# Branch a's gates started one to two heads earlier, norm factors on GpSimd and weights read in blocks, in a hybrid attention and mixture-of-experts block

## Chip, cores and metric

The kernel runs on one core of one Trainium2 chip. The metric is the device time of one execution in microseconds (us). Engines are named as in the profile: PE is TensorE, DVE is VectorE, ACT is ScalarE, POOL is GpSimd, SP is SyncE, which here only issues DMAs.

## What is computed

One layer of an encoder over L = 528 tokens (512 and 16 meta tokens) of width 1024. A normalised input `u` goes through one wide projection, its columns feed two attention branches and two gates, the gated branches are added, and a mixture of 16 experts follows.

```python
u = rms_norm(h, g_mix)
z = einsum('bld,df->blf', u, w_in)                     # 1024 x 6656
qa, ka, va, qb, kb, vb, ga, gb = split(z)
oa = diff_attention(qa, ka, va, ...)                   # 8 heads, two softmax maps each
oa = rms_norm(oa, g_subln) * (1 - lam_init)
qh = axial_rope(rms_norm(qb, g_qnorm), ...)            # 8 heads
kh = axial_rope(rms_norm(kb, g_knorm), ...)            # 2 key heads
ob = gqa_attention(qh, kh, vb)
ya, yb = oa @ w_branch_a, ob @ w_branch_b
merged = sigmoid(ga) * ya + sigmoid(gb) * yb
h = h + merged @ w_out
h = h + expert_choice_ffn(rms_norm(h, g_ffn), ...)
```

## The kernel before

**Data.** Activations lie transposed: 128 features on the partitions, 528 tokens along the free axis. Products keep float32 accuracy by splitting each factor into a high and a low part, so a projection of 128 columns is 2 halves of tokens (256 and 272) by 8 chunks by 3 products: 48 matmuls (`project`). Its weight, 128 columns of a matrix, is loaded by SP into `wraw` (`load_weights`), split by ACT into `wh` and by POOL, sometimes DVE, into `wl` (`split_weights`), one projection ahead.

**Stages.** First the input rows are normalised and transposed. Then come eight differential heads (`head_a`), then eight grouped-query heads (`head_b`), then the gates of branch b that are left, the products with `w_branch_b` and `w_out`, the routing, and the experts. While a head's scores and softmax run, PE is given projections as fill: `mix(main, fill, nfill, steps)` lets the head go on by one step when a share of the fill has been issued. A differential head is filled with the q, k and v of the next; the last one with q, v and k of the first grouped-query head. A grouped-query head h is filled with the q of the next, with the gate of branch a for block h (`gate_a(h)`) and with the product of that block with `w_branch_a` (`branch_a(h)`); the first also with the second k and v. The last one takes `gate_a(7)`, `branch_a(7)`, `gate_b(0)`; `gate_b(1)` follows, and six gates stand in the next stage.

**Order.** A recording layer (`Pace`) keeps a modelled clock for each engine and decides from it in which order instructions are written to the engines' queues. Each engine then runs its queue in order; what is late in fact is waited for, with everything behind it.

**Norm factors.** A head's output (and each q and k of branch b) is divided by a root of a mean square. `norm` sums the squares on PE (`sqh`, `sql` with `sel`), has ACT copy the sums to `rows`, has PE transpose them (`ptr<-ident,rows`), and writes mean square plus epsilon to the first column block of `cols5` (named `cols` in the profile, 128 by 5). `rsqrt` then makes the factor there: a bit trick and three Newton steps, 11 small DVE instructions. With `spread`, PE transposes the factors back across the partitions (`pz<-ident,cols`), and DVE multiplies them in. There are 18 such norms: 8 of differential heads and 2 of keys with `spread`, 8 of queries without.

**Buffers.** The tag `m1` first holds `biases` (two buffers of four rows of 528), the distance penalties of the differential heads, head h in buffer h mod 2; after the last head it is taken over for `m1`, the eight gated blocks of branch a. A gate is written by ACT to a tile of tag `f2`, a tag that the heads use too.

Of the kernel before, what the change touches and what calls it, by code (L numbers as in the profile page):

```python
# [20 lines left out]
P = 128  # L21
# [9 lines left out]
NH = 8  # L31
# [38 lines left out]
def keys(ap):  # L70

    kind = ap.name.split("_")[0]
    step = ap.ap[0][0]
    width = {"kbuf": L, "biases": 4 * L, "h2T": L, "xin": D, "pair": L, "obf": L, "hrow": D, "junk": D, "big": D, "first": D, "raw": D,
             "hid": FF // 2, "hhl": 2 * CAP, "xg": 4 * CAP}.get(kind, step)
# [187 lines left out]
class Engines:  # L263
# [7 lines left out]
    hf=1, kr=1, b0="qvkgy", b1="qgy", bn="qgy", zz="f1", bk=0, sp=0, step=6, fa=38, fa7=40, fb=40, fb2=48,  # L271
# [21 lines left out]
def block_kernel(ctx: ExitStack, tc: tile.TileContext, x, meta_tokens, g_mix, w_in,  # L293
                 lambda_q1, lambda_k1, lambda_q2, lambda_k2, g_subln, g_qnorm, g_knorm,
                 w_branch_a, w_branch_b, w_out, g_ffn, w_router, w_gate, w_up, w_down,
# [4 lines left out]
    w_in = w_in[0]  # L300
    wa, wb, wo = w_branch_a[0], w_branch_b[0], w_out[0]
# [30 lines left out]
    cols5 = [const.tile([P, 4, 5], F32, name=f"cols5{i}") for i in range(3)]  # L332
# [132 lines left out]
    def load_weights(j):  # L465
        if j < len(stream) and j not in loaded:
            w, c0 = stream[j]
# [45 lines left out]

    order = []
    for h in range(NH):
        order += [("qa", w_in, C_QA + h * P), ("ka", w_in, C_KA + h * P), ("va", w_in, C_VA + h * P)]
    cols_of = dict(q=("qb", w_in, C_QB), k=("kb", w_in, C_KB), v=("vb", w_in, C_VB))
    order += [cols_of[c] for c in K["o7"]]
    for h in range(NH):
        cols_of = dict(q=("qb", w_in, C_QB + (h + 1) * P), k=("kb", w_in, C_KB + P), v=("vb", w_in, C_VB + P),  # L520
                       g=("ga", w_in, C_GA + h * P), y=("ya", wa, h * P))
        order += [cols_of[c] for c in (K[("b0", "b1", "bn")[min(h, 2)]] if h + 1 < NH else "gy")]
    for d in range(NC):
        order.append(("gb", w_in, C_GB + d * P))
    for d in range(NC):
        order.append(("yb", wb, d * P))
    for d in range(NC):
        order.append(("wo", wo, d * P))
    stream += [(w, c) for _, w, c in order]
# [10 lines left out]
    sel = pb.tile([P, 2, P], F32R, name="sel")  # L540
    vmeta = [pb.tile([P, P], F32R, name=f"vm{i}") for i in range(2)]
# [87 lines left out]
    biases = keep.tile([P, 2, 4, L], F32, tag="m1", name="biases")  # L629
# [8 lines left out]
    nc.gpsimd.tensor_copy(ones, onef)  # L638
    for q in qmeta:
        nc.gpsimd.memset(q.bitcast(F32), 0.0)  # L640
# [105 lines left out]
    def norm(sh, sl, done, spread, sums):  # L746
# [28 lines left out]
        rsqrt(y, a, t_, c[:, 3, :])  # L775
# [264 lines left out]
    def chain(*gens):  # L1040
        for g in gens:
            yield from g

    for h in range(NH):
# [8 lines left out]
    m1 = keep.tile([P, NC, L], F32, tag="m1", name="m1")  # L1053
# [45 lines left out]
    def gate(j, tag="f2", bufs=1, place=None):  # L1099
        box = {"g": place}  # L1100

        def evac(hf, cs, ps):
            if box["g"] is None:
                box["g"] = ftile(tag, "gate", bufs)
            nc.scalar.activation(box["g"][:, cs], ps, AF.Tanh, scale=0.5)
        yield from project(j, u_h, u_l, evac)
        return box["g"]

    def gate_a(d):
        gates_b["a", d] = yield from gate(jof["ga", d], place=obf[:, NH - 1, :] if d == 0 and K["gp"] else None)  # L1110

    def branch_a(d):
        g = gates_b["a", d]

        def evac(hf, cs, ps):
# [8 lines left out]
    def gate_b(d, place=None):  # L1124
        gates_b[d] = yield from gate(jof["gb", d], *(("f0", 2) if d == 1 else ("f2", 1)), place)

    for h in range(NH):
        if h + 1 < NH:
            todo = dict(q=lambda: proj_q(h + 1), k=lambda: proj_k(1), v=lambda: proj_v(1),
                        g=lambda: gate_a(h), y=lambda: branch_a(h))  # L1130
            fill = chain(*[todo[c]() for c in K[("b0", "b1", "bn")[min(h, 2)]]])
        else:
            fill = chain(gate_a(h), branch_a(h), gate_b(0))
        mix(head_b(h), fill, K['fb2'] if h < 2 else K['fb'], K['stb'])
# [5 lines left out]
    through(gate_b(1))  # L1140
# [95 lines left out]
    places += [ftile("sqh", "gate"), ftile("f1", "gate")]  # L1236
    for d, place in enumerate(places, 2):
        through(gate_b(d, place))
# [491 lines left out]
    for i in range(4):  # L1730
# [7 lines left out]

_INS = ['x', 'meta_tokens', 'g_mix', 'w_in', 'lambda_q1', 'lambda_k1', 'lambda_q2', 'lambda_k2',
        'g_subln', 'g_qnorm', 'g_knorm', 'w_branch_a', 'w_branch_b', 'w_out', 'g_ffn', 'w_router',  # L1740
# [22 lines left out]
```

## Time and profile before

| | |
|---|---|
| median of 3 runs | 1073.41 us (1071.48 to 1073.82) |
| the profiled execution's own time | 1074.43 us |
| its span, first to last instruction | 1072.7 us |
| PE busy | 969.4 us, 90% of the span |
| DVE, ACT, POOL busy | 758.2, 630.8, 338.7 us |
| mean granted TensorE clock | 0.968 of full speed |
| DMA | 186.44 MB, 174 GB/s over the span |

The span is the time between the first and the last instruction of that execution; 1.7 us lie around it. A busy share says nothing of the end by itself: what counts is where PE, which carries most of the chain that ended last, stands idle, for whom it waits there, and at which clock it runs.

### The profile page before, as it was taken

The numbers are of one execution on the slowest core, as the hardware profiler recorded it, in microseconds if no ns is written. First come the engines' busy times: TensorE is split into PE (matmuls) and PEld (weight loads), VectorE is DVE, ScalarE is ACT, GpSimd is POOL, SyncE is SP. The second block draws the span as 40 slices with busy tenths as digits, with TensorE's granted clock in tenths as the row PEclk, the third lists the DMA queues.
The fourth block names the chain that finished last, engine by engine and source line by source line (L and its number), as shares of the span: only waits on it lengthen the run. The fifth ranks groups of instructions, "written<-read, shape, count | busy, mean of one in ns | idle before, by whom it ended". The sixth has DMA issues, their size and how long they took to land.

```text
span 1072.7 us, 18211 instructions
## 1 busy us (share of the span) xinstructions
PE 969.4 (90%) x6835; PEld 836.1 (78%) x6835; DVE 758.2 (71%) x1550; ACT 630.8 (59%) x1297; POOL 338.7 (32%) x306
## 2 busy tenths in 40 slices
PE   4799999999968999999999999985499999999984
PEld 4799998999958989999999999974256666666562
DVE  5367788887785677676656145566389999999885
ACT  5366666665745455555545433334288888888773
POOL 3232322322312322333223234432223333323153
PEclk9899999999989999999999999998699999999997
DMA  8544444443111222222222545915899999999964
GB/s 246 166 126 109 124 122 119 130 126 100 55 51 42 66 62 71 69 56 65 70 60 83 160 157 171 328 73 201 237 301 376 324 381 328 381 342 361 349 182 184
DMA packets 127502, 186.44 MB, mean 174 GB/s; under 512 B 6298, under 2 KB 84263, under 8 KB 127414
## 3 DMA queue, kind: packets, MB, share of 16 engines
q1 hardware_dynamic: 101046, 87.96, 27.5%
q0 software_dynamic: 25760, 95.16, 26.2%
q10 hardware_dynamic: 608, 2.16, 0.7%
q8 instruction: 54, 0.88, 0.3%
q14 instruction: 34, 0.28, 0.1%
HBM read 162.07 MB, written 10.76 MB: 161 GB/s over the span
## 4 chain that ended last, share of the span: by engine, by line
PE 57%; DVE 21%; ACT 9%; DMA 5%; issue 5%; SPq 1%; POOL 1%; POOLq 0%; ACTq 0%; DVEq 0%
PE pz L199 33%; PE psc L199 19%; PE ptr L199 5%; DVE sn L199 4%; DVE cols L199 3%; ACT sn L199 2%; DVE ls L199 2%; DVE pb L199 2%; SPq L199 1%; DVE wtl L199 1%; DMA raw<-in_w_down_dram 1%; DVE hl L199 1%; DVE nmb L199 1%; DVE ql L199 1%; DVE zb L199 1%
## 5 line engine op out<-in xcount | busy, mean ns | idle before, releaser
L199 POOL TENSOR_TENSOR wl<-wraw,wh 128x512 fp32r<-128x512 f32 x139 | 190.6, 1381 | 475.2 <-ACT wh L199 453.1
L199 PE MATMUL pz<-u_h,wh 128*128 128x256 f32 (+1 forms) x832 | 247.2, 297 | 5.4 <-ACT u_h L199 2.3
L199 PE MATMUL pz<-u_h,wl 128*128 128x256 f32 (+1 forms) x832 | 238.6, 287 | 1.1 <-POOL wl L199 1.1
L199 PE MATMUL pz<-u_l,wh 128*128 128x256 f32 (+1 forms) x832 | 238.4, 287 | 0.4 <-DVE u_l L199 0.4
L199 DVE TENSOR_TENSOR el<-raw,eh 128x1024 fp32r<-128x1024 f32 x180 | 214.0, 1229 | 6.0 <-ACT eh L199 4.9
L199 ACT CAST eh<-raw 128x1024 fp32r<-128x1024 f32 x180 | 182.0, 1049 | 23.5 <-PE pz L199 14.9
L199 PEld LDWEIGHTS pz<-u_h,wh 128*128 128x128 f32 x832 | 158.8, 191 | 8.3 <-DVE kbuf L199 2.7
L199 PEld LDWEIGHTS pz<-u_h,wl 128*128 128x128 f32 x832 | 158.5, 190 | 1.3 <-POOL wl L199 1.3
L199 PEld LDWEIGHTS pz<-u_l,wh 128*128 128x128 f32 x832 | 158.8, 191 | 0.6 <-DVE u_l L199 0.6
L199 PE MATMUL psc<-eh,xh 128*66 128x512 f32 (+1 forms) x272 | 105.0, 386 | 2.7 <-ACT hid L199 2.2
L199 ACT CAST wh<-wraw 128x512 fp32r<-128x512 f32 x152 | 91.0, 617 | 24.2 <-PE pz L199 10.9
L199 PE MATMUL psc<-el,xh 128*66 128x512 f32 (+1 forms) x272 | 104.1, 383 | 0.9 <-DVE el L199 0.9
L199 PE MATMUL psc<-eh,xl 128*66 128x512 f32 (+1 forms) x272 | 104.0, 382 | 0.0
L199 DVE TENSOR_TENSOR wtl<-ptr,wth 128x512 fp32r<-128x512 f32 (+1 forms) x72 | 45.9, 637 | 46.7 <-ACT wth L199 46.1
L199 ACT ACTIVATE sn<-sn,nm 128x528 f32<-128x528 f32 x64 | 47.1, 736 | 47.0 <-DVE nm L199 46.4
L199 PE MATMUL pz<-eh,hhl 128*66 128x512 f32 x224 | 70.7, 396 | 0.6 <-DVE hhl L199 0.6
L199 POOL DMA_INDIRECT acc<-ys,idxu x15 | 28.8, 1921 | 119.8 <-ACT ys L199 117.5
L199 ACT CAST wth<-ptr 128x512 fp32r<-128x512 f32 (+1 forms) x72 | 39.0, 542 | 46.0 <-PE ptr L199 45.5
L199 PEld LDWEIGHTS psc<-eh,xh 128*66 128x66 f32 x272 | 37.5, 138 | 25.4 <-ACT hid L199 3.2
L199 PEld LDWEIGHTS psc<-el,xh 128*66 128x66 f32 x272 | 37.3, 137 | 24.4 <-DVE el L199 1.4
L199 PEld LDWEIGHTS psc<-eh,xl 128*66 128x66 f32 x272 | 37.4, 138 | 21.9 <-issue 0.6
L199 DVE CUSTOM_DVE_ANT_0 sn<-psc,biases 128x528 f32<-128x528 f32 x64 | 44.3, 694 | 6.2 <-PE psc L199 6.2
(311 smaller groups left out, 2352.2 us busy)
## 6 DMA issues: line engine op xcount, KB each, us to landing
wraw<-in_w_in_dram SPq DMA_DIRECT2D x52, 512.0 KB
raw<-in_w_gate_dram POOLq DMA_DIRECT2D x13, 2048.0 KB, 18.5
raw<-in_w_down_dram POOLq DMA_DIRECT2D x13, 2048.0 KB, 15.4
raw<-in_w_up_dram POOLq DMA_DIRECT2D x13, 2048.0 KB, 20.4
biases<-in_c_bias_dram SPq DMA_DIRECT2D x8, 1056.0 KB
kbuf<-kbuf SPq DMA_DIRECT2D x32, 132.0 KB
wraw<-in_w_branch_a_dram SPq DMA_DIRECT2D x8, 512.0 KB
wraw<-in_w_branch_b_dram SPq DMA_DIRECT2D x8, 512.0 KB
```

The lines of the kernel that those rows point to most:

```text
L199: op.fn(*op.args, **op.kw)
```

## The change

1. `gate_a(0)` and `gate_a(1)` join the fill of the last differential head, behind q, v and k; its `nfill` goes from 40 to 32. A grouped-query head h then takes `gate_a(h + 1)` from head 1 on, the last takes `branch_a(7)`, `gate_b(0)`, `gate_b(1)`, and `gate_b(2)`, `gate_b(3)` follow. Four gates are left for the next stage. So block d's gate is projected one head sooner, and block 1's two heads sooner.
2. `m1` is there from the start, with `biases` as a view of it; a gate of branch a is written into the row of `m1` that `branch_a` then multiplies in place. Rows 0 and 1 lie where the even heads' penalties lay, which the last head (7) does not use.
3. `norm` calls `root` on POOL, 5 instructions: a power of -1/2 by `halfs`, and one Newton step.
4. `w_in`, `w_branch_a`, `w_branch_b` and `w_out` are put side by side on the host and cut into blocks of 128 columns, so that a partition reads 4 KB in one piece where it read 8 pieces of 512 bytes.

```diff
 K: fa7=40 -> fa7=32
+    def root(y, a, t):
+        nc.gpsimd.tensor_tensor(y, a, halfs[:, :a.shape[1]], op=OP.pow)
+        nc.gpsimd.tensor_mul(t, y, y)
+        nc.gpsimd.tensor_mul(t, t, a)
+        nc.gpsimd.tensor_scalar(t, t, -0.5, 1.5, op0=OP.mult, op1=OP.add)
+        nc.gpsimd.tensor_mul(y, y, t)
...
-            nc.sync.dma_start(raw, w[:, c0:c0 + P].rearrange("(c p) f -> p c f", p=P))
+            nc.sync.dma_start(raw, w_cols[stream[j]])
...
-    biases = keep.tile([P, 2, 4, L], F32, tag="m1", name="biases")
+    m1 = keep.tile([P, NC, L], F32, tag="m1", name="m1")
+    biases = m1.rearrange("p (a i) l -> p a i l", a=2)
...
-        rsqrt(y, a, t_, c[:, 3, :])
+        root(y, a, t_)
...
+    def gate_a(d):
+        yield from gate(jof["ga", d], place=m1[:, d, :])
...
-            fill = chain(*[dict(k=proj_k, q=proj_q, v=proj_v)[c](0) for c in K["o7"]])
+            fill = chain(*[dict(k=proj_k, q=proj_q, v=proj_v)[c](0) for c in K["o7"]], gate_a(0), gate_a(1))
...
-            nc.vector.scalar_tensor_tensor(m1[:, d, cs], g[:, cs], 1.0, ps, op0=OP.add, op1=OP.mult)
+            nc.vector.scalar_tensor_tensor(m1[:, d, cs], m1[:, d, cs], 1.0, ps, op0=OP.add, op1=OP.mult)
...
-        gates_b[d] = yield from gate(jof["gb", d], *(("f0", 2) if d == 1 else ("f2", 1)), place)
+        tags = ("f2", 1), ("f0", 2), ("sqh", 1), ("f1", 1)
+        gates_b[d] = yield from gate(jof["gb", d], *tags[d % 4], place)
...
-    through(gate_b(1))
+    through(gate_b(2))
+    through(gate_b(3))
...
+def column_blocks(*mats):
+    wide = np.concatenate([m.reshape(NC, P, -1) for m in mats], axis=2)
+    return np.ascontiguousarray(wide.reshape(NC, P, -1, P).transpose(2, 1, 0, 3))
```

**PE at the end of the last differential head.** Here `rows` are the sums of squares of the first key (their transposes), `cols` the factors, `psc<-kbh,qh` the first grouped-query scores, and `pz<-u_h,wh` a projection's matmuls. Before:

```order
L199 MATMUL pz<-u_h,wh 128x256
L199 MATMUL pz<-u_l,wh 128x256
L199 MATMUL pz<-u_h,wl 128x256
L199 MATMUL ptr<-ident,rows_93 128x128 x2
L199 MATMUL ptr<-ident,rows_93 16x128
L199 MATMUL pz<-ident,cols_82 128x128 x5
L199 MATMUL psc<-kbh_201,qh 128x264
L199 MATMUL psc<-kbl_202,qh 128x264
L199 MATMUL psc<-kbh_201,ql 128x264
L199 MATMUL psc<-kbh_201,qh 128x264
```

Now, at the key's factors (`cols_82` here):

```order
L199 MATMUL pz<-u_l,wh 128x256
L199 MATMUL pz<-u_h,wl 128x256
L199 MATMUL pz<-ident,cols_82 128x128 x4
L199 MATMUL pz<-u_h,wh 128x256
L199 MATMUL pz<-u_l,wh 128x256
L199 MATMUL pz<-u_h,wl 128x256
L199 MATMUL pz<-u_h,wh 128x256
L199 MATMUL pz<-u_l,wh 128x256
L199 MATMUL pz<-u_h,wl 128x256
L199 MATMUL pz<-u_h,wh 128x272
```

Before, the key's factors (`cols_82`) came straight behind the key's sums and the first scores straight behind the factors, with no projection between. Now 24 matmuls of the gates stand between those sums and the key's factors (the rows show the end of them), and 18 more of a gate, the last head's 26 products with its values and 12 more of a gate stand between the factors and the first scores.

**DVE and POOL in a steady differential head, at the norm of the head before.** DVE before, from the sums (`sums`) to the end of the factor:

```order
L199 TENSOR_TENSOR sums_83<-sums_83 128x5
L199 SCALAR_TENSOR_TENSOR cols_81<-sums_83,ptr 128x4
L199 SCALAR_TENSOR_TENSOR cols_81<-sums_83,ptr 16x1
L199 TENSOR_SCALAR cols_81<-cols_81 128x5 x2
L199 TENSOR_TENSOR cols_81<-cols_81 128x5 x2
L199 SCALAR_TENSOR_TENSOR cols_81<-cols_81 128x5
L199 TENSOR_TENSOR cols_81<-cols_81 128x5 x2
L199 SCALAR_TENSOR_TENSOR cols_81<-cols_81 128x5
L199 TENSOR_TENSOR cols_81<-cols_81 128x5 x2
```

POOL now, in such a head (`wl` is a weight's low part, `qmeta` a copy for the meta queries):

```order
L199 TENSOR_TENSOR wl<-wraw,wh 128x512
L199 TENSOR_TENSOR cols_82<-cols_82,halfs 128x5
L199 TENSOR_TENSOR cols_82<-cols_82 128x5
L199 TENSOR_TENSOR wl<-wraw,wh 128x512
L199 TENSOR_TENSOR cols_82<-cols_82 128x5
L199 TENSOR_SCALAR cols_82<-cols_82 128x5
L199 TENSOR_TENSOR cols_82<-cols_82 128x5
L199 TENSOR_TENSOR wl<-wraw,wh 128x512 x3
```

The 11 instructions of the root left DVE; the 5 that replace them stand on POOL among the weight splits, with one split inside the chain.

## Rows read from the trace of the kernel before

**Rows 1.** The page: its span, and the chain's shares by engine.

```profile
span 1072.7 us, 18211 instructions
...
PE 57%; DVE 21%; ACT 9%; DMA 5%; issue 5%; SPq 1%; POOL 1%; POOLq 0%; ACTq 0%; DVEq 0%
```

**Rows 2.** Busy time by stretch: bounds, length, busy (instructions) of each engine, clock, DMA.

```profile
302.05:359.32 57.27, 45.70 (x329) 42.94 (x329) 38.69 (x114) 28.91 (x74) 14.92 (x11) 0.88 0.18 50
359.32:396.06 36.74, 34.06 (x279) 33.24 (x277) 24.29 (x64) 16.67 (x42) 9.84 (x7) 1.00 0.24 68
455.40:484.54 29.14, 28.55 (x236) 27.78 (x233) 20.37 (x51) 15.98 (x42) 9.65 (x7) 1.00 0.24 65
```

**Rows 3.** PE's waits from 302 to 360 us: total, times, longest.

```profile
PE pz L199 <- DVE cols L199: 5.2, 1, 5.2
PE pz L199 <- ACT zv L199: 2.5, 1, 2.5
```

**Rows 4.** Timeline at the change of stages: start, us, engine, operation, [idle before <-releaser].

```profile
306.38 0.49 PE L199 MATMUL ptr<-ident,rows 128*128 128x128 f32 x3
...
306.78 2.48 POOL L199 TENSOR_TENSOR wl<-wraw,wh 128x512 fp32r<-128x512 f32 x2 [12.35 <-DMA zp<-zb]
...
308.11 2.43 DVE L199 TENSOR_TENSOR cols<-cols 128x5 f32<-128x5 f32 x2
...
312.09 1.09 PE L199 MATMUL pz<-ident,cols 128*128 128x128 f32 x4 [5.22 <-DVE cols L199]
```

**Rows 5.** Groups on DVE, the root's products: xcount, busy us, mean ns.

```profile
L199 DVE TENSOR_TENSOR cols<-cols 128x5 f32<-128x5 f32 x108 | 26.4, 246 | 2.0
...
L199 DVE SCALAR_TENSOR_TENSOR cols<-cols 128x5 f32<-128x5 f32 x54 | 8.8, 164 | 1.4
```

**Rows 6.** Groups on POOL, by shape.

```profile
L199 POOL TENSOR_TENSOR wl<-wraw,wh 128x512 fp32r<-128x512 f32 x139 | 190.6, 1381 | 475.2 <-ACT wh L199 453.1 <-DMA zp<-zb 14.9 <-PE ptr L199 3.0
...
L199 POOL COPY rsx<-xs 66x1 f32<-66x1 f32 x16 | 10.9, 684 | 3.7 <-DMA xs<-urow,idxu 3.7
...
L199 POOL COPY row<-cc 88x4 f32<-88x4 f32 x6 | 0.9, 180 | 2.9 <-DMA urow<-row 2.9
```

**Rows 7.** Timeline of a steady differential head, around the norm.

```profile
197.14 3.19 POOL L199 TENSOR_TENSOR wl<-wraw,wh 128x512 fp32r<-128x512 f32 x2 [7.13 <-ACT wh L199]
...
197.54 0.49 PE L199 MATMUL ptr<-ident,rows 128*128 128x128 f32 x3
197.86 1.24 DVE L199 TENSOR_TENSOR sums<-sums 128x5 f32<-128x5 f32 x1
...
203.30 0.54 PE L199 MATMUL pz<-ident,cols 128*128 128x128 f32 x3 [1.50 <-DVE cols L199]
```

**Rows 8.** PE's waits from 75 to 297 us, the steady differential heads.

```profile
PE pz L199 <- DVE cols L199: 4.5, 3, 1.5
PE psc L199 <- DVE nm L199: 4.3, 3, 1.4
```

**Rows 9.** PE's waits from 0 to 75 us.

```profile
PE psc L199 <- DMA kbuf<-kbuf: 6.7, 1, 6.7
```

**Rows 10.** Timeline of SP's DMA issues before the first scores.

```profile
42.60 0.53 SPq L199 DMA_DIRECT2D wraw<-in_w_in_dram  x1
43.23 1.95 SPq L199 DMA_DIRECT2D kbuf<-kbuf  x2
```

**Rows 11.** Busy time by stretch: small pieces of 512 bytes, and whole rows; last DMA share, GB/s.

```profile
459.00:486.00 27.00, 26.41 (x216) 25.64 (x216) 18.50 (x47) 15.00 (x40) 9.65 (x7) 1.00 0.25 69
675.00:702.00 27.00, 24.89 (x202) 23.60 (x201) 15.26 (x22) 9.98 (x24) 10.95 (x8) 1.00 0.97 330
```

**Rows 12.** Busy time by stretch: the last grouped-query head, and the gates behind it.

```profile
542.80:580.00 37.20, 36.39 (x302) 35.70 (x300) 18.23 (x41) 17.88 (x48) 8.99 (x7) 1.00 0.20 57
580.00:621.00 41.00, 39.72 (x327) 39.01 (x326) 11.86 (x20) 20.39 (x44) 14.83 (x13) 1.00 0.46 133
```

**Rows 13.** The chain that ended last, behind the last head: start, us, what.

```profile
582.64 4.86 DVE obl L199 x8
```

More of the change, by code (lines that the diff above doesn't have):

```diff
@@ L73, in keys @@
     step = ap.ap[0][0]
-    width = {"kbuf": L, "biases": 4 * L, "h2T": L, "xin": D, "pair": L, "obf": L, "hrow": D, "junk": D, "big": D, "first": D, "raw": D,
+    width = {"kbuf": L, "m1": L, "h2T": L, "xin": D, "pair": L, "obf": L, "hrow": D, "junk": D, "big": D, "first": D, "raw": D,
              "hid": FF // 2, "hhl": 2 * CAP, "xg": 4 * CAP}.get(kind, step)
@@ L292, in block_kernel @@
 @with_exitstack
-def block_kernel(ctx: ExitStack, tc: tile.TileContext, x, meta_tokens, g_mix, w_in,
+def block_kernel(ctx: ExitStack, tc: tile.TileContext, x, meta_tokens, g_mix, w_cols,
                  lambda_q1, lambda_k1, lambda_q2, lambda_k2, g_subln, g_qnorm, g_knorm,
-                 w_branch_a, w_branch_b, w_out, g_ffn, w_router, w_gate, w_up, w_down,
+                 g_ffn, w_router, w_gate, w_up, w_down,
                  g_final, c_bias, c_cos, c_sin, c_ident, c_sign, c_rev, out):
@@ L331, in block_kernel @@
     rsx = {}
-    cols5 = [const.tile([P, 4, 5], F32, name=f"cols5{i}") for i in range(3)]
+    cols5 = [const.tile([P, 3, 5], F32, name=f"cols5{i}") for i in range(3)]
     sums5 = [const.tile([P, 2, 5], F32, name=f"sums5{i}") for i in range(2)]
@@ L512, in project, with todo_b @@
             yield
+    def todo_b(h):
+        return "qvky" if h == 0 else "qgy" if h + 1 < NH else "y"
     order = []
     for h in range(NH):
-        order += [("qa", w_in, C_QA + h * P), ("ka", w_in, C_KA + h * P), ("va", w_in, C_VA + h * P)]
-    cols_of = dict(q=("qb", w_in, C_QB), k=("kb", w_in, C_KB), v=("vb", w_in, C_VB))
+        order += [("qa", 0, C_QA + h * P), ("ka", 0, C_KA + h * P), ("va", 0, C_VA + h * P)]
+    cols_of = dict(q=("qb", 0, C_QB), k=("kb", 0, C_KB), v=("vb", 0, C_VB))
     order += [cols_of[c] for c in K["o7"]]
+    order += [("ga", 0, C_GA), ("ga", 0, C_GA + P)]
     for h in range(NH):
-        cols_of = dict(q=("qb", w_in, C_QB + (h + 1) * P), k=("kb", w_in, C_KB + P), v=("vb", w_in, C_VB + P),
-                       g=("ga", w_in, C_GA + h * P), y=("ya", wa, h * P))
-        order += [cols_of[c] for c in (K[("b0", "b1", "bn")[min(h, 2)]] if h + 1 < NH else "gy")]
+        cols_of = dict(q=("qb", 0, C_QB + (h + 1) * P), k=("kb", 0, C_KB + P), v=("vb", 0, C_VB + P),
+                       g=("ga", 0, C_GA + (h + 1) * P), y=("ya", nblocks[0], h * P))
+        order += [cols_of[c] for c in todo_b(h)]
     for d in range(NC):
-        order.append(("gb", w_in, C_GB + d * P))
+        order.append(("gb", 0, C_GB + d * P))
     for d in range(NC):
-        order.append(("yb", wb, d * P))
+        order.append(("yb", nblocks[1], d * P))
     for d in range(NC):
-        order.append(("wo", wo, d * P))
-    stream += [(w, c) for _, w, c in order]
+        order.append(("wo", nblocks[2], d * P))
+    stream += [w + c // P for _, w, c in order]
     jof = {}
@@ L540, in block_kernel @@
     sel = pb.tile([P, 2, P], F32R, name="sel")
+    halfs = pb.tile([P, 5], F32, name="halfs")
     vmeta = [pb.tile([P, P], F32R, name=f"vm{i}") for i in range(2)]
@@ L638, in block_kernel @@
     nc.gpsimd.tensor_copy(ones, onef)
+    nc.gpsimd.memset(halfs, -0.5)
     for q in qmeta:
@@ L1042, in chain, with gate, evac @@
             yield from g
+    def gate(j, tag="f2", bufs=1, place=None):
+        box = {"g": place}
+        def evac(hf, cs, ps):
+            if box["g"] is None:
+                box["g"] = ftile(tag, "gate", bufs)
+            nc.scalar.activation(box["g"][:, cs], ps, AF.Tanh, scale=0.5)
+        yield from project(j, u_h, u_l, evac)
+        return box["g"]
+    def gate_a(d):
+        yield from gate(jof["ga", d], place=m1[:, d, :])
     for h in range(NH):
@@ L1048, in block_kernel @@
         else:
-            fill = chain(*[dict(k=proj_k, q=proj_q, v=proj_v)[c](0) for c in K["o7"]])
+            fill = chain(*[dict(k=proj_k, q=proj_q, v=proj_v)[c](0) for c in K["o7"]], gate_a(0), gate_a(1))
         mix(head_a(h, *got[h], biases[:, h % 2]), fill, K['fa'] if h + 1 < NH else K['fa7'], K['sta'])
     obf = keep.tile([P, NH, L], F32, tag="obf", name="obf")
-    m1 = keep.tile([P, NC, L], F32, tag="m1", name="m1")
     def head_b(h):
@@ L1097, in head_b, with branch_a @@
             Task(weigh(i, wt, combine, f"av{NH + h - 1}", finish() if i == 4 else None), Need([ls, p]), ["sn"])
-    def gate(j, tag="f2", bufs=1, place=None):
-        box = {"g": place}
+    def branch_a(d):
         def evac(hf, cs, ps):
[L1103 to L1115, printed above, removed]
-            nc.vector.scalar_tensor_tensor(m1[:, d, cs], g[:, cs], 1.0, ps, op0=OP.add, op1=OP.mult)
+            nc.vector.scalar_tensor_tensor(m1[:, d, cs], m1[:, d, cs], 1.0, ps, op0=OP.add, op1=OP.mult)
         if d == 0:
@@ L1124, in gate_b @@
     def gate_b(d, place=None):
-        gates_b[d] = yield from gate(jof["gb", d], *(("f0", 2) if d == 1 else ("f2", 1)), place)
+        tags = ("f2", 1), ("f0", 2), ("sqh", 1), ("f1", 1)
+        gates_b[d] = yield from gate(jof["gb", d], *tags[d % 4], place)
     for h in range(NH):
[L1128 to L1133, printed above, removed]
+        todo = dict(q=lambda: proj_q(h + 1), k=lambda: proj_k(1), v=lambda: proj_v(1),
+                    g=lambda: gate_a(h + 1), y=lambda: branch_a(h))
+        fill = chain(*[todo[c]() for c in todo_b(h)], *([gate_b(0), gate_b(1)] if h + 1 == NH else []))
         mix(head_b(h), fill, K['fb2'] if h < 2 else K['fb'], K['stb'])
@@ L1235, in block_kernel @@
         places += [pair[:, 0, :], pair[:, 1, :]]
-    places += [ftile("sqh", "gate"), ftile("f1", "gate")]
-    for d, place in enumerate(places, 2):
+    for d, place in enumerate(places, 4):
         through(gate_b(d, place))
@@ L1750 @@
     arrays, args = {}, []
-    feed = [(n, inputs[n]) for n in _INS] + list(shape_constants().items())
+    given = dict(inputs)
+    given["w_in"] = column_blocks(*(np.asarray(inputs[n])[0] for n in ("w_in", "w_branch_a", "w_branch_b", "w_out")))
+    feed = [(n, given[n]) for n in _INS] + list(shape_constants().items())
     for name, value in feed:
```

9 lines of the change are left out of this document (4 added, 5 removed).

## Prediction

> **What bounds the kernel now.** I read the page first: PE carries 57% of the chain that ended last and DVE 21% [rows 1], so time is lost where PE stands still for DVE. Then the busy time by stretch, cut at the meta-token scores of the last differential head (302.05 us) and of the first grouped-query heads. A steady grouped-query head takes 29.14 us for 236 matmuls, PE busy 28.55 of it at full clock [rows 2]: 123.5 ns for each matmul, with 0.6 us idle. The change of stages before it takes 57.27 us for 329 matmuls, PE busy 45.70, at a mean granted clock of 0.88 [rows 2]. At 123.5 ns those would take 40.6 us, so 16.6 us are lost there: 11.6 us idle, the rest at the lower level of the clock (1.2 instead of 2.4 GHz), to which it fell after the idle time. The next stretch loses 36.74 - 279 x 0.1235 = 2.3 us. The two lose 18.9 us.
>
> Then PE's waits: the largest in that stretch is 5.2 us for the key's factors, another 2.5 us for ACT [rows 3]. The timeline shows why: PE transposes the sums at 306.38, DVE's chain of small products is held up (two of them take 2.43 us while two weight splits run on POOL), and PE starts again at 312.09, with nothing else in its queue [rows 4]. In the steady differential heads the same wait comes in three heads, 1.5 us each, and PE waits 4.3 us in all for `nm`, also DVE's [rows 8]. At the start PE waits 6.7 us for the last shifted copies of the first keys [rows 9]. After the last head PE has no such gap: 39.72 of 41.00 us busy [rows 12].
>
> The sum is made against the profiled execution, 1074.43 us (span 1072.7 and 1.7 around it), which lies 1.0 above the median of the three runs, 1073.41.
>
> **Part 1: gates sooner.** A gate is 48 matmuls, 48 x 0.1235 = 5.9 us of PE; the two that move are 11.9 us. They leave the first grouped-query head and the stage behind the last head, both of which are PE's (0.6 us idle in a steady head [rows 2], 1.3 us in 41 [rows 12]), so those get shorter by what is taken out. They enter the stretch with 11.6 us idle. By the order, PE has 24 matmuls of gates (3.0 us) between the key's sums and factors, and 56 (6.9 us) with the last head's products between factors and first scores, where it had nothing. If the stretch then ran at a steady head's rate, all 18.9 us would go. It won't quite: the key's chain took 5.7 us from 306.38 to 312.09 [rows 4] against some 3.7 us of PE work put in its way (24 matmuls and five transposes), and three more norms with similar cover follow. I leave 1 us of wait at each of the four, in all 4: **-15 us**, with bounds -8 (every second microsecond is still waited for) and -19. Writing the gate into `m1` costs nothing: the ACT instruction and the product on DVE are the same, in another place, and the last head's penalties lie in other rows. The gates' weights are loaded and split in the same order one projection ahead; on SP they stand ahead of the key's rotated copies, so a late weight buffer would hold those. The split on POOL and ACT goes with the gate.
>
> **Part 2: factors on POOL.** DVE loses 11 instructions in each of 18 norms: the groups of 108 and 54 alone are 26.4 + 8.8 = 35.2 us of its busy time [rows 5], about 2 us a norm. An undisturbed one takes 164 ns; the mean of 246 for the two-input products comes from those that were held up while POOL ran a split, as the 1.24 us of `sums` beside the split at 197.14 shows [rows 7]. The Trainium skill, GPSIMD Engine Reference, section 1 (Specifications), says that GpSimd shares its SBUF interfaces with VectorE and contends with DVE instructions of two SBUF inputs; by that rule POOL's own small instructions will wait for DVE's in turn, and the trace agrees so far as `sums` goes.
>
> POOL gains 5 instructions a norm, each waiting for the one before. No row shows a power on POOL. Small POOL instructions take between 0.18 us (88 by 4 copy) and 0.68 us (66 by 1 copy, beside a busy DVE) [rows 6], so five are 0.9 to 3.4 us, and I take 0.45 each, 2.3 us: the power's 5 columns are few, but DVE is busy beside it. One weight split stands inside the chain in a steady differential head, 1.4 us [rows 6]. From the transposed sums to the factors that makes 1.4 us on DVE as before (197.86 to about 199.4 [rows 7]) + 2.3 + 1.4 = 5.1 us. The 1.50 us wait at 203.30 [rows 7] means that PE came to the factors 3.8 us after the sums. By the order it now has 31 or 39 matmuls between sums and factors, head by head, 3.8 or 4.8 us. So PE waits 1.3 us in one head of two and 0.3 in the other: about 6 us over seven heads, where it waited 4.5. Against that stands a DVE freer by 2 us a head, so I let 3.5 of the 4.3 us for `nm` go. Together **-2 us**. Bounds: with 0.9 us for the five the waits of rows 8 go altogether, -8.8; with 3.4 us each head waits 1.1 longer than I take, +6. In grouped-query heads the query's factors are needed a head later and only DVE's relief is left, of 0.6 us idle a head [rows 2]: **-0.5 us**, bounds +3 to -3.
>
> The Trainium skill, GPSIMD Engine Reference, section 4.1 (Engine selection), speaks against this part: elementwise arithmetic belongs on VectorE, being about twice as slow on GpSimd. By an estimate from that, four products would take 2 x 164 = 0.33 us each, 1.3 us without the power; the sum would keep its sign.
>
> **Part 3: weights in blocks.** 512 KB in 1024 pieces of 512 bytes become 128 pieces of 4 KB. A stretch with hardly anything but such pieces moves 69 GB/s at a DMA share of 0.25, 276 at full share; one with long rows moves 330 at 0.97, 340 [rows 11]. So a block takes 1.5 instead of 1.9 us. That is hidden in the heads, where DMA is busy a quarter of the time. At the start it shows: the copies PE waits for are issued at 43.23, behind a weight at 42.60 [rows 10]. Three such places lie on the path (the first weight ahead of the third input tile, and two weights ahead of the copies), 0.35 us each: **-1 us**, bounds 0 and -2.5. `halfs`, the smaller `cols5` and the packing on the host cost nothing in the chip's path.
>
> **Sum.** 1074.4 - 15 - 2 - 0.5 - 1 = 1055.9 us for an execution like the profiled one, 1 us less beside the median: I forecast **1055.5 us**.
>
> **Rivals.**
> - *POOL is late* (slower). The factor of ten norms (8 heads, 2 keys) is waited for by PE in order, with every matmul behind it. If the power took 4 us instead of 0.45, each of ten would be 3.5 us later: +35, so 1091. It decides from 18.5 + 2.1 = 20.6 us, that is 2.1 us more a norm than I take. For it: no row prices the power, and POOL's one-column copies take 0.68. Against: a product of 512 columns takes 1.4 us [rows 6], and five columns would need more than that. Chance 0.08.
> - *The chain of the first grouped-query head bounds* (less gain). Key projection, norm, rotation by DMA, split, first scores follow each other; POOL's rotation product stands ahead of the key's power in its queue. If half of the loss stays: 1074.4 - 8 - 2 - 0.5 - 1 - 1 = 1062. For it: 7 us of chain behind the key's sums. Against: a gate stands in each gap. Chance 0.17.
> - *Given back at the end.* Six gates covered the splitting of branch b's output (4.86 us on DVE [rows 13]), the reading of x and its transposes; four are left, 23.7 us. If 5 us came out from under them: 1060.5. Chance 0.08.
> - *DVE's relief is worth more*, all of rows 8 goes and the change of stages runs at a steady rate: 1074.4 - 19 - 8.8 - 1.5 - 1 = 1044, less 1. Chance 0.07.
>
> **How the numbers follow.** Forecast 0.60, rivals 0.08, 0.17, 0.08, 0.07. What a measurement of this kernel can tell from no change is about 0.2%, 2.1 us. All cases but the first rival give more than that; 0.03 of their chance goes to parts that fail together. So faster 0.89, same 0.03, slower 0.08. The range leaves out the first rival and most of the fourth, and takes in the second and third with some of part 2's upper bound: 1047 to 1067 us.
>
> **What would show it.** In the profile of the changed kernel: the granted clock stays at full speed through the change of stages and PE's waits for `zv` and for the key's factors there shrink to about 1 us; the stretch from the last differential head's meta scores to the first grouped-query head's holds some 410 matmuls in 51 to 55 us; the meta scores of steady heads stay 29.1 us apart; POOL's five are about 2.3 us a norm, and waits for `cols` name POOL; the stage behind the last head has two gates less; the wait at the start is 6 instead of 6.7 us. I am wrong if the power takes over 2 us, if PE waits more than 2 us at each factor, or if the first grouped-query head still starts behind an idle PE.

## The result, and the profile after

| | before | after |
|---|---|---|
| median | 1072.45 us (1071.03 to 1073.82, 4 runs) | 1060.18 us (1059.66 to 1060.26, 4 runs) |
| ratio of the runs | | 0.988, interval 0.9865 to 0.9896 |
| span of the profiled execution | 1072.7 us | 1058.5 us |
| PE, DVE, POOL busy | 969.4, 758.2, 338.7 us | 964.3, 726.4, 368.4 us |

The change is 12.3 us faster, where 1055.5 us were forecast: inside the range of 1047 to 1067, on the side named, and some 5 us short of the forecast. The interesting part is where those 5 us stayed.

The page after, its head and the chain's shares, answering to [rows 1]:

```profile
span 1058.5 us, 18096 instructions
...
PE 61%; DVE 14%; ACT 8%; issue 6%; DMA 5%; POOL 5%; SPq 2%; POOLq 0%; ACTq 0%; DVEq 0%
```

DVE's share of the chain fell from 21 to 14%, POOL's rose from 1 to 5%: POOL has come onto the path.

Busy time by stretch after, answering to [rows 2] and [rows 12]: from the last differential head's meta scores (the scores of the 16 meta tokens, a head's last) to the first grouped-query head's, from there to the second's, a steady grouped-query head, and, in two rows, from the seventh head's to the end of the gates that follow the last.

```profile
303.06:359.45 56.39, 52.03 (x415) 49.49 (x414) 34.32 (x76) 28.36 (x72) 24.09 (x32) 1.00 0.25 72
359.45:388.33 28.88, 28.00 (x231) 27.38 (x230) 19.87 (x38) 14.85 (x39) 10.90 (x12) 1.00 0.23 65
448.58:478.52 29.94, 28.41 (x236) 27.74 (x233) 19.07 (x41) 15.87 (x42) 11.34 (x12) 1.00 0.20 63
538.27:575.00 36.73, 35.91 (x299) 35.38 (x297) 18.10 (x42) 17.86 (x48) 9.03 (x7) 1.00 0.18 59
575.00:610.94 35.94, 35.06 (x289) 34.66 (x287) 8.75 (x19) 18.18 (x38) 13.59 (x12) 1.00 0.49 148
```

The change of stages has the clock at 1.00 where it was 0.88, with 415 matmuls in 56.39 us (410 in 51 to 55 were expected). At the steady 123.5 ns for a matmul its two stretches lose 56.39 - 51.25 = 5.1 and 28.88 - 28.53 = 0.35 us, together 5.5 where they lost 18.9: a gain of 13.4, near the 15 of the sum. The steady head, 29.14 us before, now takes 29.94 with the same 236 matmuls.

PE's waits after, in the differential heads (75 to 297 us), at the change of stages (297 to 400) and in five grouped-query heads (388.3 to 538); under them DVE's in those five heads:

```profile
PE pz L199 <- POOL cols L199: 4.7, 4, 1.2
...
PE pz L199 <- POOL cols L199: 3.3, 4, 1.4
...
PE ptr L199 <- DVE pb L199: 7.0, 5, 1.4
...
DVE cols L199 <- POOL cols L199: 5.9, 5, 1.2
```

`nm` [rows 8] is gone from the first list. At the change of stages the four factors cost 3.3 us where I left 4. The third line is the one that grew: the same five heads (396.6 to 542.8 us) waited 2.4 us for `pb` before, and 7.0 now. The fourth did not exist.

```profile
PE ptr L199 <- DVE pb L199: 2.4, 5, 0.5
```

The timeline of one such wait, a grouped-query head after, DVE and POOL with PE's last line:

```profile
468.98 0.21 DVE L199 TENSOR_SCALAR cols<-ptr 128x4 f32<-128x4 f32 x2
...
469.27 1.17 POOL L199 TENSOR_TENSOR cols<-cols,halfs 128x5 f32<-128x5 f32 x1 [2.01 <-DVE cols L199]
...
470.51 0.47 POOL L199 TENSOR_TENSOR cols<-cols 128x5 f32<-128x5 f32 x2
...
471.07 0.20 POOL L199 TENSOR_SCALAR cols<-cols 128x5 f32<-128x5 f32 x1
...
471.35 0.20 POOL L199 TENSOR_TENSOR cols<-cols 128x5 f32<-128x5 f32 x1
471.50 2.52 POOL L199 TENSOR_TENSOR wl<-wraw,wh 128x512 fp32r<-128x512 f32 x2
471.58 1.32 DVE L199 TENSOR_SCALAR cols<-cols 128x5 f32<-128x5 f32 x2 [1.18 <-POOL cols L199]
472.82 0.15 DVE L199 RECIPROCAL ls<-ls 128x1 f32<-128x1 f32 x1
473.00 1.31 DVE L199 TENSOR_SCALAR pb<-pb,ls 128x528 f32<-128x528 f32 x1
...
474.46 0.41 PE L199 MATMUL ptr<-ident,pb 128*128 128x128 f32 x2 [1.43 <-DVE pb L199]
```

POOL's five instructions take 2.3 us, from 469.27 to 471.55: the total that I took, though the power alone is 1.17 of it. PE needs nothing of the query's factors before the next head. But `done` multiplies them by `sc` and by `-sc` on DVE, and these two products stand in DVE's queue only one instruction (0.71 us, the low part of the query, not shown) behind the sums. DVE stops there for 1.18 us, and when it is released, POOL has begun the next weight split: the first of the two 128x5 products takes about 1.2 us instead of 0.16, and `pb` 1.31 instead of the 0.50 that it takes where no split runs. PE waits 1.43 us for `pb`.

The groups on POOL and DVE after, answering to [rows 5] and [rows 6]:

```profile
L199 POOL TENSOR_TENSOR cols<-cols,halfs 128x5 f32<-128x5 f32 x18 | 21.1, 1170 | 26.9 <-DVE cols L199 26.9
...
L199 DVE TENSOR_SCALAR cols<-cols 128x5 f32<-128x5 f32 x16 | 11.7, 767 | 8.1 <-POOL cols L199 8.1
L199 POOL TENSOR_TENSOR cols<-cols 128x5 f32<-128x5 f32 x54 | 11.5, 214 | 3.8
```

So I had a theory for the missing 5 us: **DVE's queue stands still for POOL**, once in each grouped-query head. The rival was that the gates' new places lengthen the heads.

To compare runs, the span is cut at five places that all of them have: the first meta-token scores of the first and the seventh differential head (A0, A6), of the second and the seventh grouped-query head (B1, B6), the first product with `w_branch_b` (Y), and the first transpose of gathered rows (X). All times are us, read from the timelines; the runs are told below:

| kernel | to A0 | A0-A6 | A6-B1 | B1-B6 (a head) | B6-Y | Y-X | span |
|---|---|---|---|---|---|---|---|
| before | 73.5 | 195.5 | 127.6 | 146.2 (29.24) | 80.2 | 142.6 | 1072.7 |
| after | 73.3 | 193.8 | 121.3 | 149.9 (29.99) | 72.7 | 140.7 | 1058.5 |
| after, again | 72.7 | 193.7 | 121.3 | 149.9 (29.97) | 72.2 | 141.9 | 1057.8 |
| gates only | 73.9 | 195.4 | 124.5 | 146.2 (29.24) | 72.6 | 141.2 | 1060.9 |
| no POOL factors | 72.4 | 195.4 | 124.4 | 146.2 (29.24) | 72.4 | 141.1 | 1059.0 |
| POOL factors but for queries | 72.9 | 193.8 | 124.0 | 146.2 (29.25) | 72.6 | 140.1 | 1057.4 |
| no blocks | 73.2 | 193.6 | 121.2 | 149.9 (29.98) | 73.9 | 142.4 | 1061.1 |
| old gates | 72.5 | 193.7 | 128.4 | 149.9 (29.98) | 79.8 | 140.0 | 1071.0 |
| old gates, products on POOL | 72.9 | 193.7 | 127.9 | 144.1 (28.83) | 80.0 | 142.4 | 1067.2 |
| products on POOL | 73.2 | 193.7 | 118.9 | 143.9 (28.79) | 72.5 | 140.5 | 1050.2 |
| true prices | 74.6 | 192.9 | 116.8 | 145.9 (29.17) | 73.0 | 141.5 | 1052.5 |
| both repairs | 73.6 | 192.9 | 116.7 | 142.4 (28.48) | 73.0 | 141.3 | 1046.7 |
| products on POOL, split outside | 74.7 | 196.1 | 120.6 | 144.1 (28.82) | 72.6 | 139.9 | 1053.8 |
| products on POOL, power alone | 73.6 | 194.1 | 123.9 | 141.9 (28.38) | 72.4 | 141.6 | 1054.2 |

A stage from A0 to Y that is untouched repeats to 0.5 us between these kernels (but for B6-Y without blocks, of which more below). The start scatters over 2.3 us and Y-X over 2.7, so no part of the change is judged by them; from X to the end all take 305.8 to 307.7 us.

### The profile page after: what moved, and what is told of

Read it like the earlier page. It is cut to its first block, busy times and chain, and to the rows that moved or that the text cites. A ratio compares the mean times of both kernels' runs of the same rounds, so it can differ in the third digit from the quotient of the medians.

```text
span 1058.5 us, 18096 instructions
## 1 busy us (share of the span) xinstructions
PE 964.3 (91%) x6835; PEld 831.8 (79%) x6835; DVE 726.4 (69%) x1354; ACT 630.2 (60%) x1297; POOL 368.4 (35%) x395
## 4 chain that ended last, share of the span: by engine, by line
PE 61%; DVE 14%; ACT 8%; issue 6%; DMA 5%; POOL 5%; SPq 2%; POOLq 0%; ACTq 0%; DVEq 0%
PE pz L199 36%; PE psc L199 19%; PE ptr L199 5%; DVE sn L199 3%; POOL cols L199 3%; ACT sn L199 2%; SPq L199 2%; DVE cols L199 1%; DVE pb L199 1%; DVE hl L199 1%; DMA raw<-in_w_down_dram 1%; DVE wtl L199 1%; DVE zb L199 1%; DVE ls L199 1%; DMA zp<-zb 1%
## 5 line engine op out<-in xcount | busy, mean ns | idle before, releaser
L199 POOL TENSOR_TENSOR wl<-wraw,wh 128x512 fp32r<-128x512 f32 x137 | 185.3, 1362 | 406.0 <-ACT wh L199 399.6
L199 DVE CUSTOM_DVE_ANT_0 sn<-psc,m 128x528 f32<-128x528 f32 x64 | 44.1, 695 | 6.7 <-PE psc L199 6.7
```

The costliest lines, as they stand in the source:

```text
L199: op.fn(*op.args, **op.kw)
```

## The experiments

### The parts undone, and done alone

**No POOL factors** (`root_dve`): the change without its third part.

```diff
...
-        root(y, a, t_)
+        rsqrt(y, a, t_, c[:, 3, :])
```

> All norm factors back on DVE (11 instructions, three Newton steps), gates and blocks as changed. Theory (DVE's queue): in a grouped-query head the two products that scale the query's factors stand on DVE behind POOL's chain, so DVE waits 1.2 us, then shares its port with a weight split, and PE waits 1.4 us for the next pb; that makes a steady grouped-query head 29.9 instead of 29.1 us. So here heads B1 to B6 come back to 29.1 to 29.3 us each (-3 to -4 us in five), the differential heads A0 to A6 lose about 1.7 us and the change of stages 1 to 2: total 1057 to 1060 us against 1060.2 for the change. Rival (the gates' new places and m1 rows lengthen the heads): heads stay at 29.9 and the total rises to 1062 to 1065.

Measured: 1061.63 us, ratio 0.9895 (0.9878 to 0.9912). The heads are back at 29.24 us, so the gates do not lengthen them: the rival falls. A0-A6 lost the 1.6 us as expected, and A6-B1 lost 3.1, more than the 1 to 2 expected; that is why the total came out above the 1057 to 1060 named. Within the change, the POOL factors thus give 1.6 + 3.1 us and take 3.7. What is left, 1 us, the medians of 1061.63 and 1060.18 do not tell from nothing: their intervals overlap.

**POOL factors but for queries** (`root_mixed`).

```diff
...
-        root(y, a, t_)
+        if spread is None:
+            rsqrt(y, a, t_, c[:, 3, :])
+        else:
+            root(y, a, t_)
```

> As the change, but the eight query norms, whose factors are not spread by PE, take their root on DVE (11 instructions); heads' outputs and keys keep theirs on POOL. Theory: grouped-query heads come back to 29.2 us each (4 us in five), the differential heads keep their gain, so 1056 to 1058 us: above the run with everything on POOL (1052), since DVE's relief is lost there. Rival (the root on DVE delays the change of stages): 1059 or more.

Measured: 1059.34 us, 0.9878 (0.9857 to 0.9898). Heads 29.25 us, and the differential heads kept their 193.8. But A6-B1 went to 124.0, as with no POOL factor at all, so the total stayed beside the change's, where the rival had it (1059 or more). So the factors on POOL shorten the change of stages by 3 us only when the queries' roots leave DVE too: the heads' and keys' alone gave 0.4 of it. Whether the queries' alone would give it, no run shows.

**Old gates** (`gates_old`): the change without its first part.

```diff
...
-    order += [("ga", 0, C_GA), ("ga", 0, C_GA + P)]
...
-            fill = chain(*[dict(k=proj_k, q=proj_q, v=proj_v)[c](0) for c in K["o7"]], gate_a(0), gate_a(1))
+            fill = chain(*[dict(k=proj_k, q=proj_q, v=proj_v)[c](0) for c in K["o7"]])
...
-                    g=lambda: gate_a(h + 1), y=lambda: branch_a(h))
+                    g=lambda: gate_a(h), y=lambda: branch_a(h))
...
```

> Branch a's gates back in their old places (gate h in head h, gate_b(0) in the last, six gates behind it), factors on POOL and blocks as changed. Theory: the gates bring the 12 us that the change of stages lost less, so 1071 to 1074, with the clock below full there again and an idle PE of 5 us or more before the key's factors. Rival (the change of stages got shorter because DVE was freed of the roots): it stays below 1066.

Measured: 1073.18 us, 1.0004 (0.9996 to 1.0013): no difference from before, so without the gates the rest of the change is worth nothing that these runs can tell. Busy time of the change of stages in this run, columns as in the first table of stretches:

```profile
299.38:357.71 58.33, 46.33 (x332) 43.23 (x329) 32.27 (x72) 28.16 (x74) 22.33 (x31) 0.88 0.17 50
```

The clock is at 0.88 again, as before [rows 2], though DVE is busy 32 us in it instead of 39. PE's wait for the key's factors came to 3.1 us, not to the 5 or more expected, and still PE is idle for 12.0 of the 58.33 us, as before (11.6). So factors on POOL do not keep PE busy there by themselves.

**Gates only** (`gates_only`): the kernel before with the gates moved and written into `m1` as in the change.

> The kernel before with the gates moved and nothing else (factors on DVE, weights as columns). If the parts simply add, undoing the gates showed 13 us, so 1059.5 here. Theory (the parts lean on each other: with the gates in place the change of stages took 124.4 us with factors on DVE against 121.3 with them on POOL): 1062 to 1066, a gain of 7 to 9 us. Stretch from the seventh head's meta scores to the second grouped-query head's: 124 to 125 us.

Measured: 1062.71 us, 0.9905 (0.9888 to 0.9922), A6-B1 124.5: inside the range expected, and a gain of 10.3 us where 7 to 9 were named. By stages it is 3.1 at A6-B1, where the extra gate of 5.9 us is done too, and 7.6 at B6-Y. The change of stages in this run, as in the first table of stretches, and PE's wait for factors (297 to 400 us):

```profile
303.33:362.59 59.26, 52.94 (x416) 51.02 (x413) 42.88 (x118) 31.11 (x78) 18.51 (x13) 0.97 0.24 68
...
PE pz L199 <- DVE cols L199: 3.3, 2, 2.8
```

The gates alone bring the clock from 0.88 to 0.97 and the longest wait for a factor there from 5.2 [rows 3] to 2.8 us; with the factors on POOL too it is 1.4, and the clock full. The parts do not add: with the gates in place the POOL factors shorten A6-B1 by 3.2 us more; without them they made it 0.8 longer (128.4 against 127.6).

**No blocks** (`no_blocks`): weights as columns again.

```diff
-            nc.sync.dma_start(raw, w_cols[stream[j]])
+            c0 = stream[j] * P
+            nc.sync.dma_start(raw, w_cols[:, c0:c0 + P].rearrange("(c p) f -> p c f", p=P))
...
```

> The four weights side by side again read as columns of 128, 1024 pieces of 512 bytes; gates and factors as changed. As predicted the blocks are worth 1 us at the start, so 1061. Theory now: the start gains nothing (the first wait for kbuf is 7.1 us with blocks, 6.7 without), and the 3 us that the routing stage got shorter (86.1 instead of 89.1 us from the first routing product to the first gathered rows' transposes) come from the blocks, since the DMA engines are full there: 1063. Rival: the blocks are worth nothing anywhere, 1060.

Measured: 1063.25 us, 0.9905 (0.9887 to 0.9922). PE's waits for the first shifted copies (0 to 75 us) and for the rows of x (540 to 612 us), without blocks:

```profile
PE psc L199 <- DMA kbuf<-kbuf: 7.2, 1, 7.2
...
PE ptr L199 <- DMA xrow<-in_x_dram: 1.6, 1, 1.6
```

and the same in the change, with them:

```profile
PE psc L199 <- DMA kbuf<-kbuf: 7.1, 1, 7.1
...
PE ptr L199 <- DMA xrow<-in_x_dram: 0.3, 1, 0.3
```

Nothing is gained at the start. The rows of x came 1.3 us earlier with blocks, but the kernel before and the one with gates only waited 0.2 for them without blocks, so this is no steady effect. My new theory put 3 us into Y-X, a stretch that scatters by as much. Against the two medians of the change the blocks are worth 3.1 and 4.2 us; the other pair that differs by them alone (no POOL factors, and gates only) says 1.1, and the intervals of all of these overlap. I leave their worth open between 0 and 4 us.

**The change again** (`after_again`): the same kernel, no edit.

> The changed kernel beside these three on one chip, so that the differences stand on the same runs: 1060 us, ratio 0.988.

Measured: 1059.06 us, 0.9873 (0.9857 to 0.989), with every stage up to Y within 0.6 us of the first profile.

### The stall in DVE's queue

**Products on POOL** (`cols_pool`): the change, with `done` on the engine that makes the factors.

```diff
-                nc.vector.tensor_scalar(cols[:, 0, :], c[:, 1, :], sc, None, op0=OP.mult)
-                nc.vector.tensor_scalar(cols[:, 1, :], c[:, 1, :], -sc, None, op0=OP.mult)
+                nc.gpsimd.tensor_scalar(cols[:, 0, :], c[:, 1, :], sc, None, op0=OP.mult)
+                nc.gpsimd.tensor_scalar(cols[:, 1, :], c[:, 1, :], -sc, None, op0=OP.mult)
```

> As the change, but the two products that scale the query's factors run on POOL too, so DVE never waits for POOL in a grouped-query head. Theory (DVE's queue): DVE's waits for cols (5.9 us over 388 to 540 us) go, PE's 1.4 us waits for pb go with them, steady grouped-query heads come to 29.1 to 29.3 us, total 1055 to 1057. Rival (POOL's chain and its weight splits hold DVE at the shared port, whoever scales the factors): heads stay at 29.7 to 29.9, total 1060.

Measured: 1052.01 us, 0.9806 (0.979 to 0.9823), better than the 1055 to 1057 of the theory, and 7 to 8 us below the two medians of the change. A steady head, by busy time:

```profile
443.75:472.45 28.70, 28.38 (x235) 27.81 (x233) 18.12 (x38) 15.95 (x42) 12.11 (x14) 1.00 0.23 66
```

and all that PE waits for in five heads, 388 to 530 us:

```profile
PE ptr L199 <- DVE pb L199: 1.1, 5, 0.2
```

DVE has no wait for POOL left there, PE's wait for `pb` fell from 7.0 to 1.1 us, and the head from 29.99 to 28.79: 1.2 us, as long as DVE's stop. How much of that was the stop and how much the held instructions behind it, the run does not separate. B1-B6 gave 6.0 us, A6-B1 2.4. The head is now 0.45 us shorter than before the change: that is DVE's relief, which the stall had hidden.

**True prices** (`priced`): the change, products on DVE, with the recording layer's costs mended.

```diff
         if self.eng == "gpsimd":
-            return 60.0 + n * 2.27
+            if self.kw.get("op") == OP.pow:
+                return 1170.0
+            return max(200.0, 60.0 + n * 2.27)
```

> As the change, but the recording layer's price of small POOL instructions is set to what the trace shows (1170 ns for the power, at least 200 ns for others, where it took some 70). It then writes the two products that scale the query's factors later into DVE's queue. Theory (DVE stands still in its queue for POOL's chain): the wait of 1.2 us a grouped-query head goes and steady heads come from 29.9 to 29.2 us or below, total 1055 to 1058. Rival (POOL's weight split behind the chain holds the two products at the shared port, wherever they stand): they still take 1.2 us and heads stay above 29.5, total 1059 to 1061.

Measured: 1051.03 us (1047.7 to 1054.33), 0.9787 (0.9763 to 0.9811). The layer had taken 60 + 5 x 2.27 = 71 ns for a power that takes 1170 and for four others that take 200 each, so it believed the factors ready 1.1 + 4 x 0.13 = 1.6 us too soon and wrote everything that needs them too early. With the true price the products stand further back. Their group in the grouped-query heads (384 to 540 us):

```profile
L201 DVE TENSOR_SCALAR cols<-cols 128x5 f32<-128x5 f32 x10 | 1.4, 164 | 0.1
```

and busy time of a steady head, and of the one that spoils the mean in the profiled execution (1054.33 us, the slowest of the five):

```profile
412.61:440.93 28.32, 28.32 (x235) 27.79 (x233) 16.52 (x45) 16.21 (x42) 10.84 (x11) 1.00 0.23 66
...
469.54:501.61 32.07, 29.98 (x235) 29.36 (x233) 14.89 (x40) 15.83 (x42) 12.48 (x12) 0.95 0.24 69
```

The products are still on DVE, and take 164 ns and wait for nothing: where they stand in the queue is the cause, not who multiplies. Four of five heads take 28.3 to 28.6 us, PE busy throughout in the one shown. The other lost 3.5: DVE waited for a rotated copy (`zp`), PE 2.09 us for `pb` behind it, and the granted clock then fell (0.95 over the head).

**Both repairs** (`priced_cols`).

> Both repairs together: the two scaling products on POOL and the recording layer's true prices for small POOL instructions. Theory: steady grouped-query heads at 28.3 us as with the prices alone, none of them with the 3.5 us that one lost there to a late rotated copy, so 1046 to 1049. Rival (what is left is PE's own work and the order's luck): 1050 to 1053.

Measured: 1048.5 us (1048.27 to 1051.83), 0.9788 (0.9771 to 0.9805), 10.6 us below the change measured again beside it. In its profile no head lost to a rotated copy. By ratio it is not to be told from true prices alone (0.9787), two of whose five runs took 1047.7 and 1048.25 us: once the prices are right, moving the products adds nothing that these runs show.

**Old gates, products on POOL** (`old_cols`): both edits above together, the gates' and the products'.

> Gates in their old places, factors on POOL and blocks as changed, and the two scaling products on POOL too. With the products on DVE this was 1073 us. Theory (the stall of DVE's queue is what ate the gain of the factors): grouped-query heads 28.8 instead of 29.9 us, total 1064 to 1067. Rival (without the gates the change of stages takes the gain back): 1069 or more.

Measured: 1068.38 us, 0.9959 (0.9945 to 0.9973): between the theory's 1064 to 1067 and the rival's 1069. The heads came to 28.83 us as the theory has it, 5.8 us less in five; Y-X, which scatters, took 2.4 more than with old gates alone. So the stall is what ate the factors' gain without the gates too.

### What is left of the wait for POOL's factors

**Split outside** (`whole_chain`), an edit to products on POOL: there, in the differential heads, PE still waits 1.15 us at four factors, and one weight split of 1.28 us stands inside POOL's five.

```diff
+        pace.prio = 0
         root(y, a, t_)
+        pace.prio = K["nrm"]
```

> As the run with the two scaling products on POOL, and the five POOL instructions of a factor are recorded at a rank that lets no weight split in between (in most differential heads the split now follows the chain). Theory: PE's four waits for POOL's factors in the differential heads (4.7 us, 1.15 us each, against the split's 1.28 us inside the chain) nearly go, so 1047 to 1050 us. Rival (another wait takes their place: the low part of the next weight is late): 1052 as without it.

Measured: 1056.52 us, 0.986 (0.9838 to 0.9883): slower than without the edit. The same place in both, products on POOL first: the power on POOL, and PE at the factors.

```profile
133.09 1.17 POOL L199 TENSOR_TENSOR cols<-cols,halfs 128x5 f32<-128x5 f32 x1 [0.42 <-DVE cols L199]
...
136.55 0.76 PE L199 MATMUL pz<-ident,cols 128*128 128x128 f32 x5 [1.12 <-POOL cols L199]
```

```profile
135.23 1.17 POOL L199 TENSOR_TENSOR cols<-cols,halfs 128x5 f32<-128x5 f32 x1 [0.41 <-DVE cols L199]
...
137.57 0.65 PE L199 MATMUL pz<-ident,cols 128*128 128x128 f32 x4 [1.27 <-POOL cols L199]
```

The chain became 1.1 us shorter (2.34 instead of 3.46 us from the power to PE), and PE waits as long as before: the recording layer puts PE's transposes where its model has the factors ready, and in this run they stand 1.27 us nearer to the power. So taking the split out of the chain does not take PE's wait out; my theory here was wrong. What would make the wait is that the model has the factors ready 1.6 us too soon, whatever stands in the chain: with true prices PE's waits for POOL's factors fell from 8.0 to 3.5 us over 75 to 660 us, which fits and does not prove it. Why the differential heads became 2.4 us longer is open; PE waits 2.0 us for `zv` (a value projection, copied by ACT) there, 0.5 without the edit.

**Power alone** (`pow_only`), also an edit to products on POOL: no Newton step.

```diff
         nc.gpsimd.tensor_tensor(y, a, halfs[:, :a.shape[1]], op=OP.pow)
-        nc.gpsimd.tensor_mul(t, y, y)
-        nc.gpsimd.tensor_mul(t, t, a)
-        nc.gpsimd.tensor_scalar(t, t, -0.5, 1.5, op0=OP.mult, op1=OP.add)
-        nc.gpsimd.tensor_mul(y, y, t)
```

> As the run with the two scaling products on POOL, but the factor is the power alone, without the Newton step: POOL's chain is 1.17 instead of some 2.2 us, and no split fits inside it. Theory: PE's waits for POOL's factors, 4.7 us in the differential heads and 3.3 at the change of stages, fall by 1 us each, eight times at most: 1044 to 1048 us. Rival (other waits take their place): 1050 to 1052.

Measured: 1055.71 us, 0.9836 (0.9811 to 0.986): the rival's side, and worse than it. The waits for POOL's factors fell from 8.0 to 3.6 us, the grouped-query heads to 28.38, but PE now waits 5.8 us for `zv` (0.8 without the edit), and A6-B1 took 5 us more, its part up to the last differential head's meta scores at a clock of 0.96 instead of 1.00. As I read it, a shorter chain changed the recorded order, and the order lost more than the chain gave; no run isolates that.

## Why the prediction was right, and where it failed

**Part 1, the gates (-15, bounds -8 and -19).** Right but for its size. The change of stages lost 18.9 us and loses 5.5, where 4 were left. The two signs came: full clock, and waits of 3.3 us at four factors where 4 were left. B6-Y got 7.5 us shorter: it has 586 matmuls instead of 642, a gate and 8 that now stand behind Y, or 6.9 us at 123.5 ns, so nothing of the gate was lost and "given back at the end" did not happen. What I did not see: the gates alone give 10.3; the last 3 us of this gain need DVE free of the queries' roots too. I had booked them under one part, so its size came as near as it did by a help that the part had not counted.

**Part 2, factors on POOL, in differential heads (-2).** Right in size: -1.7 from A0 to A6. The five instructions cost the 2.3 us that I took, shared out otherwise: 1.17 for the power, 0.2 for each of the others (0.33 by the estimate beside the sum). PE waits 4.7 us for factors (6 were forecast), 1.2 in every other head. Those for `nm` went altogether (4.3 us, where I let 3.5 go), but 1.6 us for `oa` came in, which I had not foreseen.

**Part 2, in grouped-query heads (-0.5). This is the step that failed:** "the query's factors are needed a head later and only DVE's relief is left". The first half is true of PE. But an instruction of DVE's consumes the factors at once, and a queue in order does not care who needs its result. I had asked how late PE needs the factors, and not what stands on DVE behind the two products that read them. My sign for it failed too: steady heads were to stay 29.1 us apart, and took 29.9. It cost 3.7 us in five heads; with the stall gone the same five give 2.3. That 6.0 us is more than the whole distance from the forecast.

The second half of that stall is the contention that I had read too narrowly. In the timeline above two DVE products by a scalar, which read one tile, are held beside POOL's split: a 128x5 product about 1.2 us instead of 0.16, `pb` 1.31 instead of 0.50. I had cited from the Trainium skill, GPSIMD Engine Reference, section 1 (Specifications), that DVE instructions with two SBUF inputs contend with GpSimd; the same row of that table also names those in a two-port performance mode, which would take in these scalar products if they ran in one. The trace agrees that more than two-input instructions are held; which mode they ran in, no run here shows. Not every instruction is: the reciprocal of one column at 472.82 took its 0.15 us beside the split.

The trace of the kernel before had shown it, in the stretch of [rows 4]:

```profile
307.15 0.99 DVE L199 TENSOR_SCALAR cols<-cols 128x5 int32<-128x5 int32 x2
...
309.23 1.29 POOL L199 TENSOR_TENSOR zp<-zp,sinT 128x528 f32<-128x528 f32 x1
```

The first is a scalar product on one tile, held while the first of the two splits ran. The second corrects my reading of the 2.43 us from 308.11: those two products ran beside the second split (to 309.27) and this rotation product of POOL's, not beside two splits.

**Part 3, blocks (-1).** The place was wrong: the start gained nothing, 7.1 us of wait against 6.7 [rows 9], and 7.2 without blocks. The size of a block's saving was too large as well. The queue that carries the weights, among others, took these shares of 16 engines' time, without and with blocks:

```profile
q1 hardware_dynamic: 101046, 87.96, 27.9%
...
q1 hardware_dynamic: 32950, 87.96, 26.8%
```

That is 0.279 x 1061.1 - 0.268 x 1058.5 = 12.4 us for 76 weights, 0.16 us each, where I took 0.35 from two stretches of different content [rows 11]. A third as many pieces, the same bytes, 4% less time on the queue, and no gain in the total that these runs resolve.

**The rivals.** POOL late: the power took 0.72 us more than taken, the others less, and the limit of 2.1 us more a norm was not reached; it was late, but for DVE, in a place this rival did not name. The first grouped-query head's chain: no, the stretch up to the second head's meta scores lost 0.35 us. DVE's relief worth more (1044): not in the change; with both repairs, 1048.5 is on the way there.

## What to carry to other kernels

When work moves to another engine, look for the first instruction on the old engine that reads its result: if it stands early in an in-order queue, the move has added a wait there, however late the result is really needed, so move the reader along or write it later. A planner that orders instructions by modelled costs must have the true price of a new kind of instruction; here true prices (1170 instead of 71 ns for the power, 200 for the rest) were worth some 9 us, and shortening the chain alone gave nothing in the total. And parts that fill the same gap do not add: do each alone and undo each from the whole before saying what one is worth.

## Unexpected of the hardware

A power of 128x5 on POOL takes 1.17 us where a product of that size takes 0.21 on the mean and a product of 128x512 some 1.36. A DVE instruction of one column (`nmb`) took 1.19 us instead of 0.15 beside two weight splits on POOL (products on POOL):

```profile
467.62 2.53 POOL L199 TENSOR_TENSOR wl<-wraw,wh 128x512 fp32r<-128x512 f32 x2
...
468.98 1.19 DVE L199 TENSOR_TENSOR nmb<-nmb,cols 128x1 f32<-128x1 f32 x1
```

What a held instruction loses is the rest of POOL's, not a share of its own length. In the trace of the change, nine of the 128x5 scalar products began inside a split with over 0.3 us of it left: each took 1.23 to 1.27 us and ended 0.02 to 0.03 us after that split. Seven `pb` of 128x528 that began so ended 0.29 us after theirs. Ten one-column reciprocals that began so took 0.14 to 0.16 us, as elsewhere.
